# Ten sums of the opening stretch moved from VectorE to GpSimd in a hybrid decoder trunk

## The chip, the cores and the metric

The kernel runs on one core of one Trainium2 chip. The metric is device time in microseconds (us), the median of several runs. In the profile PE is TensorE, DVE is VectorE, ACT is ScalarE, POOL is GpSimd, and SP is the engine that issues most of the DMAs. PEld is the loading of weights into TensorE.

## The reference

One decoder layer on 2048 rows of 1024 columns. What matters here is its opening: a modulation from a vector c, and a wide projection.

```python
mod = jax.nn.silu(c) @ w_ada[l] + b_ada[l]
shift, scale, gate = jnp.split(mod, 3, axis=-1)
u = x * (1.0 + scale[:, None, :]) + shift[:, None, :]
h = u @ w_in[l]
q, k, v, a_gate, p_in, p_gate, m_a, m_p = jnp.split(h, offsets, axis=-1)
...
y = jax.nn.sigmoid(m_a) * a + jax.nn.sigmoid(m_p) * p
y = (y @ w_out[l]) * (1.0 + gate[:, None, :])
x = layer_norm(DEEPNORM_ALPHA * x + y, ln_gain[l], ln_bias[l])
```

Between them stand a sliding-window attention with sinks, a multi-scale causal pool and two projections.

## The kernel before

The large products are done in blocks of two by two with seven products in place of eight (the scheme of Strassen in Winograd's form). Each side needs sums and differences of its blocks. The right side, u, is kept in "sets": B11, T1, T2, B21, T3, B22, T4, each of four pieces of 128 x 512. The left side, the weights, comes in "quads" (class `Quad`): two rows of two blocks, loaded into a tile W with four parts of 128 x 512 and a tile A (A22). A quad's sums are made in place in three calls:

- `sum1` writes part 1 as part 2 plus A22.
- `mid` makes two differences: part 1 minus part 0 into part 1, and part 0 minus part 2 into part 2.
- `late` makes one: part 3 minus part 1 into part 3.

Every operand, set or weight, is split into a high part (ACT casts it) and a low part (DVE subtracts the high part from the original), and three matmuls of high and low parts make one product. The split of two weight blocks at once is `pair_split`; it writes tiles w_set of 128 x 1024. `first`, `second` and `third` name the pairs of blocks that are split in turn: the first pair needs `sum1`, the second the first result of `mid`, the third the second result of `mid` and that of `late`.

The head (`head`) is the opening stretch. For each of eight pieces k of the input it loads modulation weights, lets PE multiply one of them with silu(c) (`pe_modulation`: 16 matmuls with one column), and DVE the other (`modulation`: the CUSTOM operation with cb, then an add of PE's sums, both into mod). Then it modulates x on ACT, makes the sets B11, T1, B21 and T2, and starts the products of the first two quads with them as the pieces come. After all eight pieces `rest_sums(i)` makes two differences for each i from 0 to 3: one for the set T3 and one for the set T4, whose piece is x of index 4 + i minus the piece ts[i]. For i = 0 and 1 they are placed at k = 6 and 7 inside the loop. The T3 set is split at the head's end, the sets B22 and T4 in hooks of the next phase (`first_phase`), between the products of the first two quads: T3, B22, then T4. In this phase `back` finishes the two quads: DVE adds of L358 and L361, gates through `consume` (L561 and L563), weight splits (L299 and L131), while POOL makes the sums of the next quads (L262, L266, L267, L271).

In the head the engines' handles are wrapped in a class that keeps the order of the program on that engine. Elsewhere a scheduler orders the instructions of each engine. Each engine takes its instructions in order, and semaphores join the engines.

Of the kernel before, what the change touches and what calls it, by code (L numbers as in the profile page):

```python
# [15 lines left out]
ALU = mybir.AluOpType  # L16
# [43 lines left out]
def kernel(  # L60
# [23 lines left out]
    pe, act, dve, pool, sp = (Ordered(tc, e) for e in (nc.tensor, nc.scalar, nc.vector, nc.gpsimd, nc.sync))  # L84
# [113 lines left out]
    def sums_to(ph, store, i, load, work=None, sums=True):  # L198

        b = []  # L200

        def x(r, c):
            return b[r][:, c * CH : (c + 1) * CH]

        def fetch():
            b.extend((ph.spare(), ph.spare()))
            b.reverse()
            for r in (1, 0):
                load(b[r], r)

        def sub(out, a, c):
            return lambda: pool.tensor_tensor(x(*out), x(*a), x(*c), ALU.subtract)

        todo = [(0, fetch)]
        if work:
            todo += [(3, lambda: work(b[0], 0)), (3.5, lambda: work(b[1], 1))]
        made = [("B11", (0, 0)), ("B21", (1, 0)), ("B22", (1, 1))] if work else []
        if work and not sums:
            made.insert(1, ("B12", (0, 1)))
        puts = [(5 + 0.6 * n, *x) for n, x in enumerate(made)]  # L220
        if sums:
            at = 7.5 if work else 4
            for out, a, c, name in (
                ((0, 1), (0, 1), (0, 0), "T1"),
                ((1, 1), (1, 1), (0, 1), "T2"),
                ((1, 0), (1, 0), (1, 1), "T4"),
                ((0, 0), (1, 1), (0, 0), "T3"),
            ):
                todo.append((at, sub(out, a, c)))
                puts.append((at + 2.5, name, out))  # L230
                at += 1.5
        for at, name, z in puts:
            todo.append((at, lambda name=name, z=z: put(sp, store, name, i, x(*z))))
        return sorted(todo, key=lambda t: t[0])
# [62 lines left out]
    def pair_split(ph, raw, a=nc.scalar, d=nc.vector):  # L297
        hi, lo = ph.split(), ph.split()
        a.copy(by_two(hi), raw)  # L299
        low(d, by_two(lo), raw, by_two(hi))  # L300
        return halves(hi, lo)
# [24 lines left out]
    def front(ph, q, tick):  # L326
        w = pair_split(ph, q.first())
        q.mid()
        a, b = bank(), bank()
        product(a, w[0], "B11", True)  # L330
        tick()
        product(b, w[1], "T1", True)
        tick()
        return a, b, None, None
# [133 lines left out]
    def steps(hooks, groups, start, todo):  # L468

        sizes = [5 * len(g) + 2 * len(n) for g, n in zip(groups, groups[1:] + [[]])]  # L470
        for offset, f in todo:
            gi, at = 0, int(start + offset)
            while at >= sizes[gi]:
                at -= sizes[gi]
                gi += 1
            hooks.setdefault((gi, at), []).append(f)
# [256 lines left out]
    def spread_bias(j):  # L733
        act.dma_start(e_rep[:, 2 * j : 2 * j + 2, :], e_d[2 * j : 2 * j + 2, :].partition_broadcast(P))
# [385 lines left out]
    def modulate(u, k):  # L1120
        dve.tensor_scalar(u, u, mod[:, 8 + k : 9 + k], mod[:, k : k + 1], ALU.mult, ALU.add)
# [20 lines left out]
    def gate_modulation(ph, m, cb):  # L1142
        wa = []

        def fetch():
            wa.append(ph.spare(ring="gate"))
            sp.dma_start(wa[0], wada[m])

        def work():
            dve.tensor_tensor_reduce(  # L1150
                wa[0], wa[0], cb, 1.0, mod[:, m : m + 1], ALU.mult, ALU.add, mod[:, m : m + 1]
            )

        return (0, fetch), (3, work)

    def head(ph, plan0):
# [22 lines left out]
        xs, ts, sums, starts = {}, {}, {}, []  # L1179
# [27 lines left out]
        def modulate_x(k):  # L1207
            for x in xs[k]:
                act.activation(x, x, AF.Identity, bias=mod[:, k : k + 1], scale=mod[:, KT + k : KT + k + 1])

        def minus(dst, a, b):
            dve.tensor_tensor(dst, a, b, ALU.subtract)

        def parts(name, i, src):
            split_set(name, i, src, eng=(act, dve))

        def opening(k):
            pe_modulation(k)
            modulation(k)

        def middle(k):

            b1, b2 = xs[k]
            if k >= 4:
                dve.scalar_tensor_tensor(ts[k - 4], ts[k - 4], sg[:, k - 4 : k - 3], b2, ALU.mult, ALU.add)
            parts("B11" if k < 4 else "B21", k % 4, b1)

        def difference(k):

            t = ts[k] = cols(ws[0][k // 2], k % 2)  # L1230
            minus(t, xs[k][1], xs[k][0])

        def closing(k):
            if k >= 4:
                parts("T2", k - 4, ts[k - 4])
                return
            hi, lo = sets["T1"][:, k, 0, :], sets["T1"][:, k, 1, :]
            scale = mod[:, KT + k : KT + k + 1]
            act.activation(hi, ts[k], AF.Copy, scale=scale)
            dve.scalar_tensor_tensor(lo, ts[k], scale, as32(hi), ALU.mult, ALU.subtract)  # L1240
            act.activation(sg[:, k : k + 1], scale, AF.Copy, scale=-1.0)

        def rest_sums(i):
            minus(xs[i][0], ts[i], xs[i][0])
            minus(xs[4 + i][0], xs[4 + i][0], ts[i])

        groups, fills, post, turn = plan0
        grp = groups[0]
        opened = [[bank(), bank(), None, None] for q in grp]

        def products(i):
            for w, (a, b, _, _) in zip(starts, opened):
                product(a, w[0], "B11", True, i, i + 1)
                product(b, w[1], "T1", True, i, i + 1)
# [12 lines left out]
        def second_pair(x):  # L1267

            o, u2 = opened[x], ph.p("u2")
            o[2:] = bank("lg"), pair_split(ph, grp[x].second(), act, dve)[::-1], u2  # L1270
            act.copy(u2, o[0])
# [8 lines left out]
        for k in range(2, KT):  # L1280
            opening(k)
            if k < 4:
                difference(k)
            if k == 7:
                second_pair(0)
            closing(k - 2)
            middle(k - 1)
            if k == 2:
                for q in grp:
                    q.sum1(dve)  # L1290
                    starts.append(pair_split(ph, q.first(), act, dve))
            modulate_x(k)
            if k in (3, 4):
                grp[k - 3].mid(dve)
            if 3 <= k < 7:
                products(k - 3)
            if k > 5:
                rest_sums(k - 6)
# [11 lines left out]
        for i in (2, 3):  # L1310
            rest_sums(i)
        late_sets(cp, "B22")
        late_sets(cp, "T3", "T4")
        for i in range(4):
            parts("T3", i, xs[i][0])
        grp[0].late(dve)
        dve.tensor_scalar(nsink, nsink, -1.0, None, ALU.mult)
        rest = [
            lambda name=name, c=c: [parts(name, i, xs[4 + i][c]) for i in range(4)]
# [4 lines left out]
    def turned(hooks, turn, gi):  # L1324
        for i in range(2):
            hooks.setdefault((gi, 1 + 2 * i), []).append(lambda i=i: turn(i))

    def first_phase(ph, plan0, opened, cb, rest):
        groups, fills, _, turn = plan0
        hooks = {}  # L1330

        def at(group, pos, f):
            hooks.setdefault((group, pos), []).append(f)

        for g in range(4):
            steps(hooks, groups, (9, 17, 25, 33)[g], fold_parts(ph, g))
        turned(hooks, lambda i: turn(ph, i), 4)
        for j in range(KT):
            at(j // 2, 3 + 5 * (j % 2), lambda j=j: spread_bias(j))
        for i in range(4):  # L1340
            ks = (i, 4 + i)
            todo = sums_to(
                ph,
                u1_d,
                i,
                lambda x, r, ks=ks: sp.dma_start(x, xt[1, ks[r]]),
                lambda x, r, ks=ks: modulate(x, ks[r]),
            )
            steps(hooks, groups, (5, 18, 31, 47)[i], todo)
        for i in range(8):  # L1350
            steps(hooks, groups, 6 + 4 * i, gate_modulation(ph, 2 * KT + i, cb))
        at(3, 0, lambda: ph.turns.clear())
        at(0, 4, lambda: groups[0][1].late(dve))
        for n, f in zip((4, 6), rest):
            at(0, n, f)
        opened_by = [q for _, _, q in fills[:2]]
        return ring(ph, groups, opened, hooks, opened_by, lambda tick: [front(ph, opened_by[0], tick)])
# [78 lines left out]
    with Pools("g0", spare=2, p=2, c=5) as ph:  # L1436
        started = head(ph, plans[0])
        kq, k, v = rooms_of("first", F32R)
# [7 lines left out]
    with Pools("g1", spare=4, p=2, c=5) as ph:  # L1446
        kq, k, v = rooms_of("second")
# [7 lines left out]
    with Pools("mix", spare=4, p=2, c=8) as ph:  # L1455
# [10 lines left out]
        for n, (raw, i) in enumerate((raw, i) for raw in (ain_d[1], pin_d[1], wo_d) for i in range(4)):  # L1466
            for offset, f in sums_to(ph, raw, i, load_raw(raw, i)):
                at = int(2 + 8 * n + offset)
                i, gi = every[at // 14]
# [78 lines left out]
```

## Time and profile before

| | |
|---|---|
| median of 3 runs | 1733.91 us (1731.9 to 1734.55) |
| the profiled execution's own time | 1734.67 us |
| its span, first to last instruction | 1732.9 us |
| its mean granted TensorE clock | 0.988 |
| busy: PE, DVE, ACT, POOL | 1665.9, 1257.8, 964.5, 1063.0 us |

How to read it. A row of the timeline gives start, length, engine, line, operation, tiles (out<-in) and shape; in brackets stands the idle time of the engine before it and what ended it. A length runs from the moment the instruction is taken up, so that of a blocked instruction holds its wait for the other engine, and two instructions in a row overlap by some 0.1 us. L56 is the line of the wrapper, so rows of the head are told apart by their tiles. A row of the table of stretches gives its length, then busy time and instructions of PE, PEld, DVE, ACT and POOL, the granted clock, the share of DMA and GB/s. A row written A:B is one of that table; other rows are of the timeline.

### The profile page before, as it was taken

How to read it: one execution, taken by the hardware profiler on the slowest of the kernel's cores; microseconds unless marked ns; L12 is line 12 of the kernel's file. 1: busy time of each engine (PE TensorE's matmuls, PEld its weight loads, DVE VectorE, ACT ScalarE, POOL GpSimd, SP SyncE). 2: the span in 40 equal slices, each digit the busy share in tenths (PEclk: the TensorE clock that was granted, in tenths of full speed). 3: DMA queues.
4: the chain of work that ended last, by engine and by line, in shares of the span. 5: the costliest groups of instructions: out<-in, count | busy, mean ns of one | idle time of the engine just before them, and what ended most of it. 6: DMA issues, size and time to landing. Idle time of an engine off the chain costs nothing.

```text
span 1732.9 us, 24692 instructions
## 1 busy us (share of the span) xinstructions
PE 1665.9 (96%) x8056; PEld 1392.2 (80%) x8056; DVE 1257.8 (73%) x2256; ACT 964.5 (56%) x2002; POOL 1063.0 (61%) x782
## 2 busy tenths in 40 slices
PE   6899999999999999999999999999999899999997
PEld 5688888888888788887888888888777678777885
DVE  5966565787778768458578777786769487859777
ACT  4544446677677654334567676765644345434552
POOL 2054427686867837862476778594656796657442
PEclk9999999999999999999999999999999899999999
DMA  9378853323433377866533334235887788786432
GB/s 352 126 287 286 222 184 110 116 100 122 153 109 98 130 260 270 286 214 206 187 110 104 131 118 152 86 117 188 313 311 260 276 299 298 268 289 234 158 142 102
DMA packets 188721, 336.79 MB, mean 194 GB/s; under 512 B 18208, under 2 KB 43952, under 8 KB 188592
## 3 DMA queue, kind: packets, MB, share of 16 engines
q1 hardware_dynamic: 185472, 330.96, 55.4%
q10 hardware_dynamic: 3088, 4.23, 1.0%
q8 instruction: 64, 1.05, 0.3%
q14 instruction: 65, 0.53, 0.1%
q0 software_dynamic: 32, 0.02, 0.0%
HBM read 227.96 MB, written 110.33 MB: 195 GB/s over the span
## 4 chain that ended last, share of the span: by engine, by line
PE 44%; POOL 7%; DVE 6%; DMA 5%; issue 4%; ACT 2%; SPq 1%; POOLq 0%; DVEq 0%; ACTq 0%
PE mm L56 28%; PE lg L56 12%; PE pv L56 2%; POOL wide L603 2%; PE pt L56 2%; DVE w_set L131 2%; POOL spare L56 1%; POOL W L262 1%; SPq L56 1%; DVE set_T L56 1%; ACT w_set L299 1%; DMA W<-in_wap_dram 1%; DMA g<-ma_d 1%; POOL W L266 1%; POOL w_set L56 1%
## 5 line engine op out<-in xcount | busy, mean ns | idle before, releaser
L56 PE MATMUL mm<-set_B,w_set 128*128 128x512 f32 x2664 | 660.1, 395 | 9.9 <-ACT w_set L299 5.2
L56 PEld LDWEIGHTS mm<-set_B,w_set 128*128 128x128 f32 x2664 | 499.1, 190 | 119.1 <-DVE w_set L131 8.4
L56 PE MATMUL mm<-set_T,w_set 128*128 128x512 f32 x1824 | 457.5, 397 | 4.5 <-POOL w_set L56 1.2
L56 PE MATMUL lg<-set_T,w_set 128*128 128x512 f32 x1728 | 424.7, 396 | 20.3 <-DVE w_set L131 8.6
L56 PEld LDWEIGHTS lg<-set_T,w_set 128*128 128x128 f32 x1728 | 326.9, 191 | 96.6 <-DVE w_set L131 14.6
L56 PEld LDWEIGHTS mm<-set_T,w_set 128*128 128x128 f32 x1824 | 337.2, 189 | 77.0 <-DVE mm L56 4.4
L131 DVE TENSOR_TENSOR w_set<-W,w_set 128x1024 fp32r<-128x1024 f32 x138 | 207.9, 1507 | 173.9 <-ACT w_set L299 164.0
L299 ACT CAST w_set<-W 128x1024 fp32r<-128x1024 f32 x138 | 144.9, 1050 | 283.1 <-PE mm L56 165.6
L56 POOL TENSOR_TENSOR w_set<-W,w_set 128x512 fp32r<-128x512 f32 x132 | 171.9, 1310 | 101.2 <-ACT w_set L56 91.3
L262 POOL TENSOR_TENSOR W<-W,A 128x512 f32<-128x512 f32 x46 | 71.5, 1554 | 218.1 <-DMA A<-in_win_dram 75.5
L56 ACT ACTIVATE L<-L,nm 128x257 f32<-128x257 f32 (+1 forms) x256 | 127.1, 498 | 26.4 <-DVE nm L56 20.3
L56 POOL TENSOR_TENSOR W<-W 128x512 f32<-128x512 f32 x82 | 108.3, 1334 | 51.6 <-DVE sm L56 30.3
L271 POOL TENSOR_TENSOR W<-W 128x512 f32<-128x512 f32 x46 | 74.7, 1624 | 98.5 <-DVE w_set L131 89.0
L56 POOL TENSOR_TENSOR spare<-spare 128x512 f32<-128x512 f32 x68 | 121.0, 1782 | 13.0 <-DMA spare<-ain_B 9.1
L56 DVE CUSTOM_DVE_ANT_0 L<-lg,bt,nsink 128x256 f32<-128x256 f32 (+1 forms) x256 | 111.6, 473 | 20.4 <-DMA bt<-e_rep 9.4
L56 ACT CAST w_set<-W 128x512 fp32r<-128x512 f32 (+1 forms) x164 | 100.1, 626 | 38.2 <-POOL W L56 25.7
L56 DVE COPY o<-pv 64x256 f32<-64x256 f32 x128 | 54.3, 424 | 81.1 <-PE pv L56 79.8
L56 ACT CAST pth<-pt 128x512 fp32r<-128x512 f32 (+1 forms) x128 | 72.8, 568 | 63.3 <-PE pt L56 62.9
L56 ACT ACTIVATE L<-L,sm 128x256 f32<-128x256 f32 (+1 forms) x128 | 64.3, 503 | 68.1 <-DVE sm L56 67.8
L266 POOL TENSOR_TENSOR W<-W 128x512 f32<-128x512 f32 x44 | 75.0, 1705 | 34.2 <-DVE w_set L131 25.1
L267 POOL TENSOR_TENSOR W<-W 128x512 f32<-128x512 f32 x44 | 74.4, 1691 | 31.6 <-DMA W<-in_win_dram 26.0
L56 DVE TENSOR_SCALAR L<-L,sm 128x256 f32<-128x256 f32 (+1 forms) x128 | 89.9, 702 | 0.0
(225 smaller groups left out, 2468.3 us busy)
## 6 DMA issues: line engine op xcount, KB each, us to landing
W<-in_win_dram SPq DMA_DIRECT2D x42, 512.0 KB, 5.5
W<-in_win_dram SPq DMA_DIRECT2D x42, 256.0 KB, 3.7
A<-in_win_dram SPq DMA_DIRECT2D x42, 256.0 KB, 4.6
ag_d<-sig SPq DMA_DIRECT2D x32, 256.0 KB, 5.1
pg_d<-sig SPq DMA_DIRECT2D x32, 256.0 KB, 4.6
pg<-pg_d SPq DMA_DIRECT2D x32, 256.0 KB, 3.1
pin_B<-fin SPq DMA_DIRECT2D x32, 256.0 KB, 2.1
ag<-ag_d SPq DMA_DIRECT2D x32, 256.0 KB, 2.8
```

The lines of the kernel that those rows point to most:

```text
L56: return lambda *args, **kw: self.tc.keep_in_program_order(op(*args, **kw))
L131: engine.tensor_tensor(dst, src, as32(hi), ALU.subtract)
L262: e.tensor_tensor(self.w[:, 1, :], self.w[:, 2, :], self.a22, ALU.add)
L266: e.tensor_tensor(x[:, 1, :], x[:, 1, :], x[:, 0, :], ALU.subtract)
L267: e.tensor_tensor(x[:, 2, :], x[:, 0, :], x[:, 2, :], ALU.subtract)
L271: e.tensor_tensor(x[:, 3, :], x[:, 3, :], x[:, 1, :], ALU.subtract)
L299: a.copy(by_two(hi), raw)
L603: nc.gpsimd.tensor_tensor(dst, g, dst, ALU.add)
```

## The change

Ten element-wise operations of 128 x 512, all float32 with two inputs and one output in SBUF, are issued on GpSimd in place of VectorE. They are named here in the order in which they stand on GpSimd:

- P1 and P2: `mid` of the first quad, P3 and P4: `mid` of the second.
- R0, R1, R2 and R3: the second difference of `rest_sums(0)` to `rest_sums(3)`, that for T4.
- L0 and L1: `late` of the first quad and of the second.

On GpSimd they stand behind the last step of the bias rows and ahead of the sums of the next two quads (L262), one directly behind the other. The scheduler also changes a few places outside the head: on VectorE the low part of the first quad's third pair (L131) comes directly behind the first add of L358, and on SyncE some loads and stores of the next phase change places.

```diff
-        def minus(dst, a, b):
-            dve.tensor_tensor(dst, a, b, ALU.subtract)
+        def minus(dst, a, b, e=dve):
+            e.tensor_tensor(dst, a, b, ALU.subtract)
...
         def rest_sums(i):
             minus(xs[i][0], ts[i], xs[i][0])
-            minus(xs[4 + i][0], xs[4 + i][0], ts[i])
+            minus(xs[4 + i][0], xs[4 + i][0], ts[i], pool)
...
             if k in (3, 4):
-                grp[k - 3].mid(dve)
+                grp[k - 3].mid(pool)
...
-        grp[0].late(dve)
+        grp[0].late(pool)
...
-        at(0, 4, lambda: groups[0][1].late(dve))
+        at(0, 4, lambda: groups[0][1].late(pool))
```

## The prediction

> **What bounds the kernel now.** The page first: which engine is full over the span. Then the table of busy time in stretches, for the head alone, where the change lies.
>
> ```profile
> span 1732.9 us, 24692 instructions
> PE 1665.9 (96%) x8056; PEld 1392.2 (80%) x8056; DVE 1257.8 (73%) x2256; ACT 964.5 (56%) x2002; POOL 1063.0 (61%) x782
> ...
> 40.00:60.00 20.00, 19.20 (x100) 16.08 (x100) 19.33 (x33) 14.29 (x24) 0.00 (x0) 0.91 0.12 46
> 60.00:80.00 20.00, 15.58 (x61) 12.12 (x60) 18.58 (x27) 11.18 (x19) 3.11 (x2) 0.91 0.53 171
> ...
> 100.00:120.00 20.00, 20.00 (x111) 17.43 (x111) 9.43 (x11) 7.64 (x12) 9.16 (x6) 1.00 0.65 201
> ```
>
> TensorE (PE) fills the span, so the head is worth the time at which PE stops waiting. From 40 to 80 VectorE (DVE) is full while GpSimd (POOL) does almost nothing; from 100 PE is busy 20.00 of 20. The timeline shows where PE waits in between, and for whom.
>
> ```profile
> 59.17 0.69 DVE L56 TENSOR_TENSOR head_kk<-head_kk,head_B 128x512 f32<-128x512 f32 x1
> 59.78 0.69 DVE L56 TENSOR_TENSOR x<-head_B,x 128x512 f32<-128x512 f32 x1
> ...
> 63.39 0.68 DVE L56 TENSOR_TENSOR W<-W 128x512 f32<-128x512 f32 x1
> 64.07 0.69 DVE L358 TENSOR_TENSOR lg<-lg,u 128x512 f32<-128x512 f32 x1
> 66.26 0.70 DVE L361 TENSOR_TENSOR mm<-lg,p 128x512 f32<-128x512 f32 x1 [0.31 <-ACT p L359]
> 67.02 0.73 PE L56 MATMUL lg<-set_T,w_set 128*128 128x512 f32 x2 [2.84 <-DVE mm L361]
> 68.07 1.21 DVE L131 TENSOR_TENSOR w_set<-W,w_set 128x1024 fp32r<-128x1024 f32 x1
> 69.20 0.68 DVE L56 TENSOR_TENSOR W<-W 128x512 f32<-128x512 f32 x1
> 69.34 4.03 PE L56 MATMUL lg<-set_T,w_set 128*128 128x512 f32 x10 [1.58 <-DVE w_set L131]
> 73.20 2.91 PE L56 MATMUL mm<-set_B,w_set 128*128 128x512 f32 x12
> 73.40 0.69 DVE L383 TENSOR_TENSOR p<-lg,p 128x512 f32<-128x512 f32 x1 [1.11 <-PE lg L56]
> 87.22 3.94 DVE L131 TENSOR_TENSOR w_set<-W,w_set 128x1024 fp32r<-128x1024 f32 x2
> 88.99 2.60 PE L56 MATMUL mm<-set_B,w_set 128*128 128x512 f32 x10 [0.93 <-DVE w_set L131]
> ```
>
> Each PE wait here ends on DVE; 88.99 is the last before PE is full. So what DVE gains or loses up to about 73 is the kernel's. The price of a moved operation on DVE is 0.6 us (59.17 to 59.78, start to start).
>
> **What the move costs DVE.** This view shows both engines when POOL wakes up.
>
> ```profile
> 75.50 1.49 POOL L262 TENSOR_TENSOR W<-W,A 128x512 f32<-128x512 f32 x1 [56.69 <-DMA A<-in_win_dram]
> 75.74 1.80 DVE L56 TENSOR_TENSOR set_T<-x,set_T 128x512 fp32r<-128x512 f32 x1
> 77.07 1.62 POOL L267 TENSOR_TENSOR W<-W 128x512 f32<-128x512 f32 x1
> 77.47 1.77 DVE L56 TENSOR_TENSOR set_T<-head_vv,set_T 128x512 fp32r<-128x512 f32 x1
> 85.41 1.28 DVE L56 CUSTOM_DVE_ANT_0 first_vv<-first_vv,cb,mod 128x1024 f32<-128x1024 f32 x1
> 85.52 2.33 POOL L262 TENSOR_TENSOR W<-W,A 128x512 f32<-128x512 f32 x1 [6.83 <-DVE sig L563]
> 130.06 2.32 DVE L56 CUSTOM_DVE_ANT_0 first_vv<-first_vv,cb,mod 128x1024 f32<-128x1024 f32 x1
> ```
>
> The two set_T operations, 0.69 alone, take 1.80 and 1.77 beside POOL. They end at 77.54 and 79.24, 1.70 apart: 0.60 of DVE's own and 1.10 in which POOL's operation runs and DVE stands. At 85.41 it is POOL that stands until DVE is done; at 130.06 a DVE product of 1.28 takes 2.32. So the two take turns, instruction by instruction, and a POOL operation put into a full stretch of DVE costs it 1.10 where it saves 0.60. The Trainium skill says this outright (SBUF — State Buffer, "Who interferes with whom"): a VectorE instruction with two SBUF inputs and a GpSimd instruction that reads SBUF exclude each other for the whole instruction, and issue order decides who stands. By that rule the change pays only where DVE waits anyway; the rows agree, with 1.10 as its price here.
>
> So each of the ten costs DVE between -0.60 (wholly inside a wait of DVE) and +0.50: all ten together between -6.0 and +5.0. The waits decide which.
>
> ```profile
> 25.39 3.57 PE L56 MATMUL lg<-ct,head_T 128*128 128x1 f32 x16 [0.37 <-DMA head_T<-in_wadat_dram]
> 29.98 0.69 DVE L56 TENSOR_TENSOR W<-W,A 128x512 f32<-128x512 f32 x1
> 31.78 1.23 DVE L56 TENSOR_TENSOR w_set<-W,w_set 128x1024 fp32r<-128x1024 f32 x1 [1.11 <-ACT w_set L56]
> 32.92 1.28 DVE L56 CUSTOM_DVE_ANT_0 head_T<-head_T,cb,mod 128x1024 f32<-128x1024 f32 x1
> 34.79 0.75 DVE L56 SCALAR_TENSOR_TENSOR set_T<-head_B,mod,set_T 128x512 fp32r<-128x512 f32 x1
> 36.06 1.29 DVE L56 TENSOR_TENSOR W<-W 128x512 f32<-128x512 f32 x2
> 37.43 0.85 PE L56 MATMUL mm<-set_T,w_set 128*128 128x512 f32 x3
> 39.51 1.84 PE L56 MATMUL pt<-ct,head_T 128*128 128x1 f32 x16
> 45.95 0.15 DVE L56 TENSOR_TENSOR mod<-mod,lg 128x1 f32<-128x1 f32 x1 [0.46 <-PE lg L56]
> 50.52 0.15 DVE L56 TENSOR_TENSOR mod<-mod,lg 128x1 f32<-128x1 f32 x1
> 50.59 1.22 DVE L56 TENSOR_TENSOR w_set<-W,w_set 128x1024 fp32r<-128x1024 f32 x1
> ...
> 34.99:38.40 3.41, 3.41 (x25) 3.10 (x24) 3.41 (x5) 2.66 (x5) 0.00 (x0) 1.00 1.03 408
> 48.64:52.05 3.41, 2.61 (x20) 2.16 (x19) 3.29 (x6) 2.82 (x5) 0.00 (x0) 1.00 0.00 0
> 52.05:55.46 3.41, 3.41 (x9) 2.59 (x9) 3.41 (x7) 2.53 (x5) 0.00 (x0) 0.50 0.00 0
> 69.10:72.50 3.40, 3.16 (x8) 2.49 (x9) 3.19 (x6) 2.58 (x5) 0.00 (x0) 0.50 0.64 213
> ```
>
> **Step 1, the middle sums P1 to P4.** P1 waits for the first quad's low half; it gets its turn when the sum of 29.98 is done (30.6) and fits into the 1.11 in which DVE waits for ACT: free. P2 queues behind the low half of 31.78 and holds up the product of 32.92; P3 holds up the difference behind that product; P4 holds up the SCALAR_TENSOR_TENSOR of 34.79. Three blocks, 3.3; the pair of sums at 36.06 (1.2) goes, and so does its twin for the second quad, one row of mod later (1.2). DVE is 2.1 late before the twin's place and about 0.8 late behind it.
>
> **Step 2, who waits for that.** The operation of 34.79 writes the low half of T1, which ended at 35.54 and now ends near 38.8. PE's second matmul of row 37.43 wants it at 37.66: PE stands 1.1, where it had no gap. What this does to PE's clock is the unknown. At 52.05 the granted clock is 0.50 for 3.4 us, after a stretch (48.64) in which PE had sixteen one-column matmuls, two full ones and a gap. The stretch from 34.99 would now look alike: sixteen one-column matmuls, four full ones, a gap. So I take half clock from 38.4 to 41.8, where a full matmul takes 0.43 (4.03 for 10 at 69.34) and not 0.23: seven of them, +1.4, PE +2.5 in all. The Trainium skill (TensorE: Matmul & The Clock Gate, Part 1) lets the clock fall after at least one idle window of about 3.4 us. By that rule a gap of 1.1 costs no clock, and the sum below would be 2.5 in place of 3.0; row 52.05, behind a gap of 0.8 (48.64: 2.61 busy of 3.41), speaks against it.
>
> DVE needs PE's one-column sums at every mod row, and waited there already (45.95, 0.46). With PE at +1.1, DVE sets the pace: 0.8, plus 0.55 for R0 (half of its 1.10 falls into that wait), minus 0.6 for its saving, plus 1.10 for R1, minus 0.15 of waits gone: +1.7 at 50.59. With PE at +2.5, the mod rows wait for PE and hide more of R0: +2.6. I take +2.6.
>
> **Step 3, from 50.59 to 64.07.** DVE has no gap there. R2, R3, L0 and L1 follow each other on POOL, each taking its turn between two DVE operations: +4.4. DVE loses R1, R2, R3 and L0 from its own order: -2.4. So +2.0; the add of 64.07 comes at +4.6, 68.65. L0 is ready by then: ACT's cast of the third operands needs it and stands behind four T3 casts, so it hides L0's lateness.
>
> **Step 4, given back.** DVE's order of the changed program is different behind that add: the low half of row 68.07 now follows it directly, and L1 (69.20) is gone. Before PE's T3 product had all it needs, 64.07 to 69.28 passed; now add, low half, gate and L361 take 0.6 + 1.13 + 0.6 + 0.6 = 2.95. T3 starts whole at 71.6, in place of two matmuls at 67.02 and ten from 69.34. DVE's own seven operations up to the row of 73.40 end at 71.6 + 4.2 = 75.8 (+2.4). PE's twelve matmuls take 5.2 at half clock (76.8, +3.4), which follows such a gap (69.10, 0.50), and 2.9 at full. Half clock lasts 3.4 us, so it ends within them: +3.0.
>
> **Step 5, the rest.** From 73.40 to 87.22 DVE keeps its operations and its two or three turns with POOL; PE is released by it at 88.99, and from 100 on is full. The +3.0 is carried to the end; another fall of the turns is worth up to two blocks, 1.2 net either way. POOL's own queue stood empty for 56.69 before 75.50, so the ten delay nothing behind them. On SP a store of a gate now stands ahead of a load of the next weights; POOL's sums of 75.50 and 77.07 wait for such loads, but they end at 78.7 and DVE's reader of them is at 87.22, so a delay of several microseconds is hidden.
>
> Sum: +3.0 on the median 1733.91 gives 1736.9 (the profiled execution, span 1732.9, itself took 1734.67, 0.8 above the median; by it 1737.7). It is 0.17%; 0.2%, 3.5 us, is about what a measurement of this kernel can tell from no change.
>
> **Rivals.**
> *No exclusion in the head.* If POOL's work there cost DVE nothing, P1 to P4 and R0 would still save nothing, since the sum of 50.52 follows PE's; R1, R2, R3 and L0 save 2.4, step 4 gives T3 whole at 61.7 + 2.95 = 64.6, and DVE's next seven end at 68.8 in place of 73.40: -4.6, 1729.3. The rows of 75.74 to 130.06 are against it; they lie behind the head, which is all that is for it. 0.10.
> *Cover.* The blocks fall mostly into waits of DVE, as P1 does, and step 4 pays the others: 0 to 1 late, 1734.4. DVE's 19.33 of 20 leaves little room. 0.10.
> *Half clock twice.* If the stretch 38.4 to 41.8 does not count as busy, the next one is half too: the sixteen one-column matmuls take 3.57 (25.39) and not 1.84, three full ones 0.6 more. PE is late by another 2.4, DVE's mod rows wait for it: +5.4, 1739.3. It decides as soon as PE loses more than about 0.4 of that stretch (69.10 was 3.16 of 3.40 busy and was followed by full clock). 0.20.
> *Full clock at step 2* is inside the forecast: +1.7 there, and +1.6 (DVE) to +2.5 (PE) at 73.40.
> That the ten stay on DVE is excluded: the changed program's order has ten fewer on DVE and ten more on POOL.
>
> **Numbers.** Forecast, +1.6 to +4.2 with step 5's 1.2: 0.60, two fifths of it above 3.5. Slower: 0.24 + 0.20 = 0.44. Same: 0.36 + 0.10 = 0.46. Faster: 0.10. The range leaves out no-exclusion and the tail of half clock twice: from 1733.0 (cover, turns falling well) to 1740.0.
>
> **What would show it.** Right: DVE operations beside the ten that last 1.8 in place of 0.69, POOL operations of up to 2.3; a PE wait for set_T near 37.7; T3 whole near 71.6; the release of 88.99 near 92. Wrong: ten short POOL operations with DVE rows unchanged beside them, or T3 before 67.

## The result and the profile after

The changed kernel takes 1743.92 us, the median of 6 runs (1741.89 to 1747.1), against 1734.23 of six runs of before beside it (1731.9 to 1735.48): ratio 1.0058, 95% interval 1.0048 to 1.0068, or 9.7 us slower. The forecast was 3.0 slower, with a range up to 1740.0. The direction was right, the size was not.

The page of after, its profiled execution took 1743.75:

```profile
span 1742.0 us, 24693 instructions
PE 1668.0 (96%) x8056; PEld 1392.8 (80%) x8056; DVE 1257.3 (72%) x2246; ACT 964.2 (55%) x2002; POOL 1072.9 (62%) x792
```

The busy times hardly move: DVE loses ten operations and half a microsecond, so what it saves it gives back in longer rows. PE's 9.1 us of span are 2.1 more busy time and 7 more waiting. Where that arises is found by taking one event after the other in both timelines. First the opening of after, around P1 to P4. The rows in this and the other fences are picked from the timeline, in order of time:

```profile
30.09 2.90 POOL L56 TENSOR_TENSOR W<-W 128x512 f32<-128x512 f32 x2 [11.56 <-DVE w_set L56]
31.72 2.35 DVE L56 TENSOR_TENSOR w_set<-W,w_set 128x1024 fp32r<-128x1024 f32 x1 [1.12 <-ACT w_set L56]
34.12 0.80 PE L56 MATMUL mm<-set_B,w_set 128*128 128x512 f32 x1 [1.14 <-DVE w_set L56]
35.26 1.68 DVE L56 TENSOR_TENSOR head_B<-x 128x512 f32<-128x512 f32 x1
36.00 3.41 PE L56 MATMUL pv<-ct,head_T 128*128 128x1 f32 x16
36.87 1.75 DVE L56 SCALAR_TENSOR_TENSOR set_T<-head_B,mod,set_T 128x512 fp32r<-128x512 f32 x1
...
43.25 1.47 PE L56 MATMUL mm<-set_T,w_set 128*128 128x512 f32 x3
44.53 1.86 PE L56 MATMUL pt<-ct,head_T 128*128 128x1 f32 x16
46.43 0.15 DVE L56 TENSOR_TENSOR mod<-mod,pt 128x1 f32<-128x1 f32 x1 [3.47 <-PE pt L56]
```

The same place of the timeline of before, rows that the prediction did not show:

```profile
33.65 1.46 PE L56 MATMUL mm<-set_T,w_set 128*128 128x512 f32 x3
34.93 1.86 PE L56 MATMUL pv<-ct,head_T 128*128 128x1 f32 x16
42.21 0.15 DVE L56 TENSOR_TENSOR mod<-mod,pt 128x1 f32<-128x1 f32 x1
```

The low half of the second quad takes 2.35 in place of 1.23: it stands for P2. PE waits 1.14 for it at 34.12. Up to here PE is at half clock in both kernels (three matmuls in about 1.47: 0.43 each). Before leaves it at about 34.9: its sixteen one-column matmuls take 1.86. After does not: there they take 3.41, and the full matmuls are still at 0.43 in the row of 43.25. Full clock comes with the row of 44.53, which began at 39.51 in before: PE is 5.0 late. Then the rest of the head, and the next phase:

```profile
55.83 1.21 DVE L56 TENSOR_TENSOR w_set<-W,w_set 128x1024 fp32r<-128x1024 f32 x1
65.45 3.47 DVE L56 TENSOR_TENSOR x<-head_B,x 128x512 f32<-128x512 f32 x2
71.32 0.69 DVE L358 TENSOR_TENSOR lg<-lg,u 128x512 f32<-128x512 f32 x1
74.40 5.01 PE L56 MATMUL lg<-set_T,w_set 128*128 128x512 f32 x12 [4.67 <-DVE mm L361]
79.44 0.69 DVE L383 TENSOR_TENSOR p<-lg,p 128x512 f32<-128x512 f32 x1 [0.91 <-PE lg L56]
82.87 0.69 DVE L563 TENSOR_TENSOR sig<-sig,mm 128x512 f32<-128x512 f32 x1 [1.00 <-ACT sig L561]
84.57 1.34 POOL L262 TENSOR_TENSOR W<-W,A 128x512 f32<-128x512 f32 x1 [16.20 <-DMA W<-in_win_dram]
84.68 3.48 DVE L56 TENSOR_TENSOR set_T<-head_kk,set_T 128x512 fp32r<-128x512 f32 x2
89.76 1.48 POOL L262 TENSOR_TENSOR W<-W,A 128x512 f32<-128x512 f32 x1 [2.15 <-ACT sig L561]
90.01 1.79 DVE L563 TENSOR_TENSOR sig<-sig,p 128x512 f32<-128x512 f32 x1
91.72 1.77 DVE L56 TENSOR_SCALAR spare<-spare,mod 128x1024 f32<-128x1024 f32 x1
93.41 0.67 DVE L563 TENSOR_TENSOR sig<-sig,mm 128x512 f32<-128x512 f32 x1
94.01 1.15 DVE L131 TENSOR_TENSOR w_set<-A,w_set 128x512 fp32r<-128x512 f32 x1
95.22 4.14 PE L56 MATMUL lg<-set_T,w_set 128*128 128x512 f32 x10 [2.75 <-DVE w_set L131]
99.20 2.88 PE L56 MATMUL mm<-set_B,w_set 128*128 128x512 f32 x12
```

And of before, three rows of the same work, where PE has no such waits:

```profile
82.29 5.31 PE L56 MATMUL lg<-set_T,w_set 128*128 128x512 f32 x22 [0.29 <-DVE w_set L131]
84.21 0.68 DVE L131 TENSOR_TENSOR w_set<-A,w_set 128x512 fp32r<-128x512 f32 x1
84.81 0.68 DVE L563 TENSOR_TENSOR sig<-sig,mm 128x512 f32<-128x512 f32 x1
```

Starts of the same events, where no end is named (the rows of before are here and in the prediction):

| event | before | after | late by |
|---|---|---|---|
| PE's sixteen columns into pt | 39.51 | 44.53 | 5.0 |
| add of pt to mod | 42.21 | 46.43 | 4.2 |
| low half of the first quad's second pair, end of the mod rows | 50.59 | 55.83 | 5.2 |
| first add of L358 | 64.07 | 71.32 | 7.25 |
| row p, L383 | 73.40 | 79.44 | 6.0 |
| last low part of A (L131), released to PE | 84.21 | 94.01 | 9.8 |
| the product that was released at 88.99, its end | 91.59 | 102.08 | 10.5 |
| the span's end | 1732.9 | 1742.0 | 9.1 |

So two steps up carry the result: 5 us before 46, and 4 us between 79 and 95. What lies between and behind them is smaller (+2.0, -1.2 and, at the end, -1.4). In the second step POOL's sums of the next quads (84.57 to 93) meet the last T4 parts, a gate, a scaling and the low part of A on DVE; in before these sums ran at 75.50 and 77.07 beside other T4 parts, while PE had products, and again from 85.52, behind the low part of 84.21.

### The profile page after: what moved, and what is told of

It is laid out like the page before. It is cut to its first block, busy times and chain, and to the rows that moved or that the text cites. A ratio compares the mean times of both kernels' runs of the same rounds, so it can differ in the third digit from the quotient of the medians.

```text
span 1742.0 us, 24693 instructions
## 1 busy us (share of the span) xinstructions
PE 1668.0 (96%) x8056; PEld 1392.8 (80%) x8056; DVE 1257.3 (72%) x2246; ACT 964.2 (55%) x2002; POOL 1072.9 (62%) x792
## 4 chain that ended last, share of the span: by engine, by line
PE 40%; POOL 8%; DVE 7%; DMA 6%; issue 5%; ACT 2%; SPq 1%; POOLq 0%; DVEq 0%; ACTq 0%
PE mm L56 26%; PE lg L56 11%; DVE w_set L131 2%; PE pv L56 2%; POOL wide L603 2%; PE pt L56 2%; DMA spare<-pin_B 1%; POOL spare L56 1%; DMA W<-in_wap_dram 1%; POOL W L262 1%; DMA set_B<-pin_B 1%; POOL nxt L56 1%; DMA g<-mp_d 1%; POOL w_set L56 1%; DVE set_T L56 1%
## 5 line engine op out<-in xcount | busy, mean ns | idle before, releaser
L131 DVE TENSOR_TENSOR w_set<-W,w_set 128x1024 fp32r<-128x1024 f32 x138 | 201.9, 1464 | 182.0 <-ACT w_set L299 169.9
L262 POOL TENSOR_TENSOR W<-W,A 128x512 f32<-128x512 f32 x46 | 70.0, 1522 | 175.4 <-DMA W<-in_win_dram 40.0
L56 POOL TENSOR_TENSOR W<-W 128x512 f32<-128x512 f32 x88 | 118.6, 1362 | 64.4 <-DVE w_set L56 32.0
L271 POOL TENSOR_TENSOR W<-W 128x512 f32<-128x512 f32 x46 | 74.8, 1626 | 103.7 <-DVE w_set L131 91.2
L266 POOL TENSOR_TENSOR W<-W 128x512 f32<-128x512 f32 x44 | 75.1, 1709 | 39.8 <-DVE w_set L131 30.8
L267 POOL TENSOR_TENSOR W<-W 128x512 f32<-128x512 f32 x44 | 74.0, 1681 | 34.9 <-DMA W<-in_win_dram 29.2
```

What stands on the lines that cost most here:

```text
L56: return lambda *args, **kw: self.tc.keep_in_program_order(op(*args, **kw))
L131: engine.tensor_tensor(dst, src, as32(hi), ALU.subtract)
L262: e.tensor_tensor(self.w[:, 1, :], self.w[:, 2, :], self.a22, ALU.add)
L266: e.tensor_tensor(x[:, 1, :], x[:, 1, :], x[:, 0, :], ALU.subtract)
L267: e.tensor_tensor(x[:, 2, :], x[:, 0, :], x[:, 2, :], ALU.subtract)
L271: e.tensor_tensor(x[:, 3, :], x[:, 3, :], x[:, 1, :], ALU.subtract)
```

## The experiments

Ratios are to runs of before on the same chip: 1735.52 (35 runs) for the first four kernels, 1735.55 (24) for the next four, 1735.7 (21) for the last three. A thousandth is 1.7 us.

**The ten write a constant.** This asks what the change would bring if POOL's ten operations did not hold DVE. It leaves out the ten differences.

```diff
-            minus(xs[4 + i][0], xs[4 + i][0], ts[i], pool)
+            pool.memset(xs[4 + i][0], 0.5)
...
-                grp[k - 3].mid(pool)
+                [pool.memset(grp[k - 3].w[:, p, :], 0.5) for p in (1, 2)]
...
-        grp[0].late(pool)
+        pool.memset(grp[0].w[:, 3, :], 0.5)
...
-        at(0, 4, lambda: groups[0][1].late(pool))
+        at(0, 4, lambda: pool.memset(groups[0][1].w[:, 3, :], 0.5))
```

> The ten operations of GpSimd write a constant into the same tiles in place of a difference of two: they read no SBUF, stand in the same places, and every other instruction of every engine is that of the changed kernel. Left out of the computation: the ten differences. Theory A (turns: a GpSimd operation that reads SBUF and a VectorE operation with two SBUF inputs exclude each other, and what is lost goes on into TensorE's clock): the 1.68, 1.75, 2.30, 2.35 of VectorE's rows beside the ten become 0.69, 0.75, 1.28, 1.23, TensorE has full clock from about 35 as before, the add of L358 comes near 62 in place of 71.3, and the time is at or below that of before, by 0 to 6 us (1728 to 1734), less what the changed order of the next phase costs. Theory B (the loss comes from the order of the next phase, which this kernel keeps, not from the ten): about 1739 to 1744. Theory C (the ten are late for their readers on ACT because GpSimd is slow): in between, about 1738, as a constant is written faster than a difference is made.

It took 1734.37, ratio 0.9992 (0.9981 to 1.0004). Its timeline:

```profile
29.86 0.98 POOL L56 MEMSET W<- 128x512 f32 x2 [12.68 <-DVE w_set L56]
31.50 1.23 DVE L56 TENSOR_TENSOR w_set<-W,w_set 128x1024 fp32r<-128x1024 f32 x1 [1.11 <-ACT w_set L56]
57.86 1.29 DVE L56 TENSOR_TENSOR x<-head_B,x 128x512 f32<-128x512 f32 x2
61.55 0.69 DVE L358 TENSOR_TENSOR lg<-lg,u 128x512 f32<-128x512 f32 x1
65.51 3.03 PE L56 MATMUL lg<-set_T,w_set 128*128 128x512 f32 x12 [1.40 <-DVE mm L361]
83.25 3.96 PE L56 MATMUL lg<-set_T,w_set 128*128 128x512 f32 x10 [3.05 <-DVE w_set L131]
```

DVE's rows are as short as when alone (1.23, and 1.29 for two, where after has 2.35 and 3.47), PE has no wait at 34, and the add of L358 comes 2.5 before that of the kernel before, 9.8 before that of after. All of the loss up to there comes from the ten operations, not from the order of instructions. A constant is also written faster than a difference (0.49 against 1.1), so the ten are ready sooner here; but in after no wait of PE, ACT or DVE between 25 and 100 ends on POOL, so it is the turns and what follows from them that cost. The Trainium skill (SBUF — State Buffer, "Who interferes with whom") says that a VectorE instruction with two SBUF inputs does not contend with a GpSimd instruction that only writes SBUF; these rows agree. But of what the head gains little arrives: row p (L383) comes 3.6 before that of before (69.80), the last low part of A 2.55 (81.66), with PE waiting 3.05 for it at 83.25. The later loss is there even without the first, though smaller.

**Each group of moves alone.** In each the other two groups go back to VectorE.

The middle sums alone, against the changed kernel:

```diff
-            minus(xs[4 + i][0], xs[4 + i][0], ts[i], pool)
+            minus(xs[4 + i][0], xs[4 + i][0], ts[i], dve)
...
-        grp[0].late(pool)
+        grp[0].late(dve)
...
-        at(0, 4, lambda: groups[0][1].late(pool))
+        at(0, 4, lambda: groups[0][1].late(dve))
```

> Only P1 to P4 on GpSimd, the other six on VectorE as before; the order of all else is that of before. Theory A: GpSimd's P2 holds up the low half of the second quad (2.35), TensorE waits for it at 33 and stays at half clock until about 46, VectorE waits for TensorE's one-column sums of k = 5 by 3.5; the add of L358 comes 4 to 5 later than before and stays so: +4 to +5 (1738 to 1739). Theory B: no change, as the order is that of before (1734). A third, that the middle sums cost only their turns (3 blocks of 1.1 less 2.4 saved) without the clock: +1.

The set differences alone:

```diff
-                grp[k - 3].mid(pool)
+                grp[k - 3].mid(dve)
...
-        grp[0].late(pool)
+        grp[0].late(dve)
...
-        at(0, 4, lambda: groups[0][1].late(pool))
+        at(0, 4, lambda: groups[0][1].late(dve))
```

> Only R0 to R3 on GpSimd; the order of all else is that of before. Theory A: four blocks of 1.1 less four savings of 0.6, R0's half hidden in a wait for TensorE: +1.4 to +2 (1735.6 to 1736.2), no change of clock before 50. Theory B: no change (1734). No exclusion: -1.8 (1732.4).

The last sums alone:

```diff
-            minus(xs[4 + i][0], xs[4 + i][0], ts[i], pool)
+            minus(xs[4 + i][0], xs[4 + i][0], ts[i], dve)
...
-                grp[k - 3].mid(pool)
+                grp[k - 3].mid(dve)
```

> Only L0 and L1 on GpSimd; with it VectorE's order behind the adds of L358 changes somewhat, though not as in the changed kernel, and GpSimd does L0 and L1 as soon as the second pair is split, near 52 to 58. Theory A: two blocks of 1.1 less 0.6 at the add of L358, +1.6, then L1 gone from VectorE in front of the T3 product's next splits, -0.6: +1 (1735). Theory B (order of the next phase): +3 to +4 by that alone, 1737 to 1738. No exclusion: -1.2 (1733).

The middle sums alone: 1739.88, 1.0023 (1.0013 to 1.0034). The differences alone: 1735.59, 1.0000 (0.9990 to 1.0009). The last sums alone: 1736.4, 1.0004 (0.9995 to 1.0012). The timeline of the middle sums alone:

```profile
31.53 2.35 DVE L56 TENSOR_TENSOR w_set<-W,w_set 128x1024 fp32r<-128x1024 f32 x1 [1.12 <-ACT w_set L56]
33.93 0.51 PE L56 MATMUL mm<-set_B,w_set 128*128 128x512 f32 x1 [1.25 <-DVE w_set L56]
34.28 0.87 PE L56 MATMUL mm<-set_T,w_set 128*128 128x512 f32 x3
34.98 2.62 PE L56 MATMUL pv<-ct,head_T 128*128 128x1 f32 x16
42.71 1.84 PE L56 MATMUL pt<-ct,head_T 128*128 128x1 f32 x16
44.59 0.15 DVE L56 TENSOR_TENSOR mod<-mod,pt 128x1 f32<-128x1 f32 x1 [1.82 <-PE pt L56]
```

A row of the table of stretches of the same run, with the granted clock behind POOL's column:

```profile
35.85:42.65 6.80, 6.80 (x21) 5.73 (x21) 6.80 (x9) 5.04 (x10) 2.02 (x2) 0.50 0.95 376
```

The 2.35 and PE's wait are as in after, but PE had reached full clock just before (0.87 for three at 34.28), lost it within the sixteen columns and was back at 42.71: 3.2 late, not 5.0. DVE waits 1.82 for it and not 3.47. The groups alone cost 4.0, 0 and 0.7 us by their ratios, 4.7 together; the whole costs 9.7. So about half of it belongs to no group alone.

**The next quads' sums write a constant**, in after and in the kernel with the ten constants. This asks for the share of the second step. It leaves out four sums (L262 and L267 of the next two quads).

```diff
-            self.srcs, self.consume, self.ahead = srcs, consume, ahead
+            self.srcs, self.consume, self.ahead = srcs, consume, ahead; self.flat = False
...
-            e.tensor_tensor(self.w[:, 1, :], self.w[:, 2, :], self.a22, ALU.add)
+            e.memset(self.w[:, 1, :], 0.5) if self.flat else e.tensor_tensor(self.w[:, 1, :], self.w[:, 2, :], self.a22, ALU.add)
...
-            e.tensor_tensor(x[:, 2, :], x[:, 0, :], x[:, 2, :], ALU.subtract)
+            e.memset(x[:, 2, :], 0.5) if self.flat else e.tensor_tensor(x[:, 2, :], x[:, 0, :], x[:, 2, :], ALU.subtract)
...
+        groups[1][0].flat = groups[1][1].flat = True; grp = groups[0]
```

> The changed kernel, and in it the four sums of the next two quads that GpSimd makes near 84 to 93 (L262 and L267, twice) write a constant and read no SBUF; every other instruction stands where it stands in the changed kernel. Left out of the computation: those four sums. Turns theory: up to the second quads' B22 products all is as in the changed kernel (about +6 on before); then VectorE's rows of 1.7 to 1.8 near 85 to 94 become 0.7 to 0.8, the splits for the two T4 products come without delay, TensorE's waits of 1.4 and 2.8 there shrink to below 1 and half clock near 96 is gone: +6 and not +9.7 on before, 1741 to 1742 where the changed kernel would have 1745. Order theory (VectorE's, ACT's and SyncE's changed order costs by itself): no change, 1745.

> As the kernel whose ten operations write constants, and in it the four sums of the next two quads write constants too. Left out of the computation: the ten differences and these four sums. Turns theory: that kernel was 4.8 ahead of before at the end of the T3 product and only 1.5 ahead at the start of the next quads; without the four reads it keeps 4 to 5 of it: about 1731 where before has 1735.5. Order theory: 1.5 ahead as it was, 1734.

After with these four: 1738.32, 1.0026 (1.0014 to 1.0038). Its timeline:

```profile
34.39 0.86 PE L56 MATMUL mm<-set_T,w_set 128*128 128x512 f32 x3
74.39 0.53 POOL L267 MEMSET W<- 128x512 f32 x1 [2.37 <-DMA W<-in_win_dram]
77.34 0.69 DVE L383 TENSOR_TENSOR p<-lg,p 128x512 f32<-128x512 f32 x1 [0.51 <-PE lg L56]
82.58 1.29 DVE L56 TENSOR_TENSOR set_T<-head_kk,set_T 128x512 fp32r<-128x512 f32 x2
88.61 0.68 DVE L131 TENSOR_TENSOR w_set<-A,w_set 128x512 fp32r<-128x512 f32 x1
89.34 2.60 PE L56 MATMUL lg<-set_T,w_set 128*128 128x512 f32 x10 [0.68 <-DVE w_set L131]
```

From row p to the last low part of A pass 11.27 here (77.34 to 88.61), 14.57 in after, 10.81 in before. So the four sums take 3.3 of the time between these two in after. In before their turns there, on the T4 parts of 75.74 and 77.47, take 2.2, so not all of the 3.3 is new. And part of this kernel's lead over after is not theirs: up to 60 its instructions are those of after, yet PE was at full clock around its wait (0.86 for three at 34.39), as in the middle sums alone, and the add of L358 came at 69.62, 1.7 sooner than in after. The ten constants together with the four: 1731.67, 0.9981 (0.9972 to 0.9990). That is what could be had if none of this POOL work held DVE. It also leaves out what the four sums cost in before, which no run measured alone; with the four sums in their place it is 0.9992.

**P2 and P4 back on VectorE**, from before and from after: P1, by the prediction's reading, is free.

```diff
-        def mid(self, e=nc.gpsimd):
+        def mid(self, e=nc.gpsimd, e2=None):
...
-            e.tensor_tensor(x[:, 2, :], x[:, 0, :], x[:, 2, :], ALU.subtract)
+            (e2 or e).tensor_tensor(x[:, 2, :], x[:, 0, :], x[:, 2, :], ALU.subtract)
...
+                grp[k - 3].mid(pool, dve)
```

> Only the first operation of each of the two middle sums (P1 and P3) on GpSimd, the second (P2 and P4) on VectorE; the order of all else is that of before. Theory that P2 does the harm, by taking its turn ahead of the low half of the second quad so that TensorE's clock stays half: P1 falls into VectorE's wait for ACT and is free, the low half takes 1.23 again, TensorE's wait at 33 is gone and full clock comes at 35; P3 costs one block of 1.1, the two savings are 1.2: 0 to -0.5 (1735 to 1735.5). Theory that any of the middle sums on GpSimd delays T1 enough for TensorE's clock: +2 to +4 (1737.5 to 1739.5).

> The changed kernel with P2 and P4 back on VectorE, so eight of the ten on GpSimd; the order of ACT and SyncE is that of the changed kernel. Theory that P2's turn and the clock are 4 to 5 of the loss: full clock from 35, no wait of VectorE for TensorE of 3.5 at k = 5, the add of L358 near 67 and not 71.3: +5 on before, 1740 to 1741. Theory that the next phase makes up for whatever comes early or late (its own waits set the end): 1743 to 1745, as the changed kernel.

Only P1 and P3 moved: 1734.29, 0.9991 (0.9981 to 1.0001). After without P2 and P4: 1740.62, 1.0033 (1.0021 to 1.0046). The timelines, P1 and P3 alone first:

```profile
31.54 1.23 DVE L56 TENSOR_TENSOR w_set<-W,w_set 128x1024 fp32r<-128x1024 f32 x1 [1.12 <-ACT w_set L56]
34.23 1.84 PE L56 MATMUL pv<-ct,head_T 128*128 128x1 f32 x16
```

```profile
66.31 0.69 DVE L358 TENSOR_TENSOR lg<-lg,u 128x512 f32<-128x512 f32 x1
81.31 3.44 DVE L56 TENSOR_TENSOR set_T<-head_kk,set_T 128x512 fp32r<-128x512 f32 x2
86.80 3.02 PE L56 MATMUL lg<-set_T,w_set 128*128 128x512 f32 x12 [3.24 <-DVE w_set L131]
91.03 2.56 PE L56 MATMUL lg<-set_T,w_set 128*128 128x512 f32 x10 [1.21 <-DVE w_set L131]
```

Without P2 the low half is 1.23, PE doesn't wait, and full clock is there for the sixteen columns (1.84). In after without P2 and P4 the first step is gone: the add of L358 is 2.2 late, not 7.25. It is still 5.7 us slower than before, since PE now waits 3.24 and 1.21 for the low parts of A, and two T4 parts take 3.44. The two steps are separate: either can be taken away, and the other stays. Without the first 5.7 us are left of 9.7, with the four sums constant 4.5 (1.0026); the two gains, 4.0 and 5.2, make up about the whole.

**Repeats, and one more selection** (P1, P3 and R0: this edit on top of the one that moves P1 and P3 from before).

```diff
-            minus(xs[4 + i][0], xs[4 + i][0], ts[i])
+            minus(xs[4 + i][0], xs[4 + i][0], ts[i], pool if i == 0 else dve)
```

> The changed kernel itself, once more, for two questions. Its time: 9 to 11 us over before on this chip too if the placing decides (ratio 1.005 to 1.0065). Its opening stretch: the first profile had two stretches of half clock behind the wait at 34.1, two kernels with the same instructions up to 60 had one. If the phase of the clock's stretches against the program decides (it is not set by the kernel), this profile may show one or two, with the add of L358 near 69.6 (one) or 71.3 (two); if the number of stretches belongs to this program, two again, 71.3. In either case the low half behind quad 2's cast takes 2.35 and the next quads' sums fall on the last operations of T4.

> Only P1 and P3 on GpSimd, once more, since its first interval touched 1. If it gains what its profile showed (0.5 to 1.4 us), the ratio is 0.9992 with an interval below 1; if that was chance, 1.000.

> P1, P3 and R0 on GpSimd, the other seven on VectorE. If R0 falls into VectorE's wait for TensorE at the add to mod of k = 5 (0.46 long in before), it takes at most 0.6 off VectorE: up to 0.6 us faster than P1 and P3 alone, 0.9988. If it holds the product or the split beside it for 1.10, VectorE is 0.5 later from there, and the time is that of before, 1.000.

The changed kernel again: 1744.09, 1.0042 (1.0028 to 1.0055). P1 and P3 again: 1735.12, 0.9998 (0.9989 to 1.0007). P1, P3 and R0: 1735.02, 0.9995 (0.9985 to 1.0004). So the slowing holds, with 7 to 10 us as its size, and no selection that was tried is shown to beat the kernel before: the 0.9991 of P1 and P3 did not come again. The second profile of after:

```profile
43.20 1.30 PE L56 MATMUL mm<-set_T,w_set 128*128 128x512 f32 x3
71.13 0.69 DVE L358 TENSOR_TENSOR lg<-lg,u 128x512 f32<-128x512 f32 x1
```

Up to the add of L358 at 71.13 it agrees with the first to 0.2 us, with half clock up to the row of 43.20; PE's wait for the last low part of A ends at 95.39, after 3.26.

## Why the prediction missed

In the prediction's own sum, +3.0 became +9.8 at the last low part of A: 2.6 more in step 2, 0.4 less given back in step 4, and 3.8 gathered in step 5, which was put at nothing, within 1.2.

**Step 1, failed in P2's place.** The number of blocks was right: P3 and P4 hold the difference of 35.26 (1.68) and the operation of 36.87 (1.75), as foretold. P2 was put behind the low half of 31.78 and got its turn ahead of it. DVE waits there for ACT's cast until 31.7. P1 began when the sum of 29.91 was done (30.6) and needs 1.1, so it ended as the cast came, with P2 next on POOL; both were done at 32.99 (30.09 and 2.90), and the rest of the 2.35, to 34.07, is the low half's own time. The prediction used that gap for P1 and forgot that P2 stands ready at its end. The price is the 1.1 foretold, but it holds the operand that PE wants next, and not a product that feeds mod.

**Step 2, failed in size, for that reason.** PE's wait came at 33.0 to 34.1, not near 37.7, and there PE is still at half clock. The forecast was one stretch of half clock, +2.5 for PE. Measured: half clock on to 44.5, +5.0. The rival *half clock twice* had that price (2.5 and another 2.4 for PE; the sixteen columns at 3.57, measured 3.41), from another place: there full clock is lost, here it is not reached. It was given 0.20, and its time of 1739.3 is still 4.6 short, since it too carried the delay unchanged through step 5. So +5.2 stood where +2.6 was foretold, at the row of 50.59. That P2's turn causes this is shown by the two kernels without P2 and P4, where wait and half clock are both gone; P4, which begins behind the wait, can't have caused it.

The same wait cost PE 3.2 in the middle sums alone and in after with four constants 3.3 (its sixteen columns into pt stand at 42.84), where full clock had come just ahead of it, and 5.0 in both profiles of after, where it had not. The instructions up to there do the same work in all four, so it isn't their order that decides this; what does is not settled, as no experiment moved it. The prediction's 0.43 for a matmul at half clock is right, though its row (4.03 for 10) doesn't give it: full clock is back at 72.50, within that row.

Behind the rows on the clock one rule was weighed: a gap of 1.1 costs no clock, since the clock falls only after an idle window of about 3.4 us (the Trainium skill, TensorE: Matmul & The Clock Gate, Part 1). The middle sums alone go from 0.87 for three matmuls to a granted clock of 0.50 from 35.85 to 42.65, with no gap beyond 1.25 near it. So the row spoke truer than the rule; here a wait and sixteen one-column matmuls are enough.

**Step 3, right.** +2.0 was foretold between 50.59 and 64.07; 5.24 to 7.25 is +2.0. Its four turns stand in the rows, two of them in 65.45.

**Step 4, right.** A return of 1.6 was foretold (+4.6 to +3.0) and 1.2 measured (7.25 to 6.04). T3 starts whole, 3.08 behind the add of L358 (71.32 to 74.40), where 2.95 was foretold (its four terms add up to 2.93). Half clock ended within its twelve matmuls (5.01, foretold 5.2 at most). In part this was luck: half clock lasted not 3.4 but 6.8 (0.50 from 71.90 to 78.65), and began 2.5 ahead of the product.

**Step 5, failed.** "The +3.0 is carried to the end", within 1.2. Measured: +3.8 between row p and the last low part of A. The prediction saw that POOL's next sums wait for loads, and asked only whether *their reader* gets them in time. It didn't ask on whom their turns would fall. In before the first two turns fall on T4 parts that PE needs late, and the next begin at 85.52, behind the low part of A of 84.21; the low part that they hold there, at 87.22, releases PE at 88.99 after a wait of 0.93. In after all four come between 84.57 and 93, ahead of the low part of A, which is at 94.01. The bound, two blocks or 1.2 net, was too small. From row p to the start of the last low part of A, turns took 2.2 in the row of 84.68 (3.48 for two, 1.28 alone), 1.1 at 90.01 and 1.0 at 91.72: 4.3 in place of the 2.2 that the T4 parts of 75.74 and 77.47 paid before. A wait for a gate at 82.87 took 1.0 more, and a gate (93.41) that in before stands behind the low part (84.81) another 0.6: 3.7 of the 3.8. So 1.6 of it is no turn. What brings these sums so late is in part a load (the sum of 84.57 is released by that of W), in part the 6.0 that all is late by; the two were not taken apart.

**The rival *no exclusion*** was tried by the ten constants: T3 whole 65.51, with 64.6 foretold, and row p at 69.80, with 68.8 foretold, so its reading of the head was nearly right. But its -4.6 ended as -1.4 by the ratio, with an interval that holds no change, in part because of step 5 again: PE's wait of 3.05 at 83.25; with the four sums constant too it was -3.3. That the sign of the forecast was right has the reason given: DVE stands for POOL's operations where it is full.

Of the signs listed, the long DVE rows and the longer POOL rows were there. PE's wait for set_T near 37.7 was not; it was for w_set at 34.12. T3 came at 74.40, not 71.6, and the product that was released at 88.99 began, whole, at 99.20, not near 92.

## What to carry to other kernels

When an operation moves to an engine that takes turns with the old one, don't only count turns: ask for each which instruction of the other engine is next *and ready* at that moment, and whether PE waits for that one; here one turn of 1.1 ahead of PE's next operand, P2's, made PE 5.0 late, and the four set differences alone cost nothing that could be measured (1.0000). A delay isn't carried through a later stage unchanged if that stage has turns of its own: shift its rows by the delay and look at what the turns, and the order of the instructions, now put ahead of PE's next operand. Ask of a short PE wait what it does to the clock: a wait of 1.14 cost 5.0 here, one of 1.25 cost 3.2.

## What the runs showed of the hardware

- A POOL operation of 128x512 that reads two inputs makes DVE's row beside it 1.1 longer when its turn comes first. One that writes a constant leaves DVE's rows as they were and takes 0.49 (0.98 for two) to 0.53, with exceptions: at 85.24 in after with four constants it took 1.01, beside a scaling TENSOR_SCALAR of 84.98 (0.80), so there it was POOL that stood.
- Not only operations with two inputs were held: the scaling TENSOR_SCALAR of 128x1024 took 1.77 (91.72) beside POOL's sums, and 0.80 alone (89.28).
- The column of the granted clock doesn't show the opening's half clock in after. For the stretch in which sixteen columns take 3.41 the table of stretches says 1.00 (the column behind POOL's). The trace's records of the clock begin only when full clock comes, at 44.57 in after, and the column counts what lies ahead of them as 1.00; in the middle sums alone, whose records begin before the wait, it says 0.50. So the spacing of the matmuls is what to read there:

```profile
34.90:38.30 3.40, 3.40 (x16) 3.11 (x14) 3.40 (x5) 1.32 (x2) 3.17 (x2) 1.00 1.04 410
```
